# Differential attention: low weight parts made by an accumulating DMA, and one reciprocal for two sums

## The chip, the cores and the metric

The program runs on one core of a Trainium2 chip. The metric is the device time of one execution in microseconds (us), as the median of several. The engines are named as the profile names them: PE (TensorE, matrix products), DVE (VectorE), ACT (ScalarE), POOL (GpSimd) and SP (SyncE, which issues most DMAs). PEld is PE's loading of weights, which overlaps with its products.

## The reference, cut to what matters

The model has four layers over 512 latent and 256 context tokens of width 1024. A layer is a token mixer and a squared-ReLU MLP. The mixer of layer 1, the second, is differential attention, and the change is in it alone. It has 8 heads with two softmax maps each:

```
s1 = q1 @ k1.T * scale;  s2 = q2 @ k2.T * scale        # q, k with rotary positions for latent tokens
p  = softmax(s1) - lam * softmax(s2)                   # lam: one learned scalar
o  = p @ v                                             # v is 128 wide per head
y  = (rms_norm(o, subln_g) * (1 - lam_init)) @ w_o
```

Latent queries attend to all 768 keys, context queries to the 256 context keys. Everything is in float32.

## The kernel before, in words

**Products in two parts.** Each float32 operand is split into a high part (a cast to the matrix engine's 32-bit format fp32r) and a low part (what the cast left out), and a product is three products: high by high, high by low, low by high (`mm3g`, L147). `split` (L95) makes the parts: the ACT casts (`hi`, L96), and the DVE subtracts the high part from the source (`lo`, L97). Weights come from HBM into a raw buffer, issued by SP, and are then split (`wload` L99, and `gload` L111 with a pool of its own for four tiles `g`).

**The stage.** `diff` (L803) works on head after head. Its weights are loaded in tiles of 128x512. A pool of eight tiles (tag `w`) holds four pairs of parts; raw tiles have two buffers. The weights of a value projection (`gen_v`, L841, for two heads at a time) are four pairs, those of a key projection (`loads`, L895) two, those of the output projection (`gen_wo`, L911) four one after the other; those of a query projection go through `gload`. For each head and block of 128 queries `S` (L929) makes the scores of both maps in PSUM and then the softmax: the DVE takes the row maximum (L948), the ACT the exponential with its row sum `li` (L949), the DVE the reciprocal (L950) and its product with `lam` (L952); the ACT scales the second map (L953) and the DVE combines the two (L954). `Tr` transposes them, `PVa` and `PVb` multiply by the values and normalise.

**What sets the order.** PE's order is written out by hand. The object `Fill` (L163) holds the projections as generators in a queue (`v0`, `q1`, `k2`, ...), and between the steps of the attention `F(ns)` runs as many of their products as fit. `prime` (L184) starts the loads of the next generator in the queue early. A load takes the next buffers of the pool in turn, so it has to wait until the last product that reads the buffers' former tile. DVE, ACT, POOL and SP get their order from a scheduler when the program is built; each runs its instructions strictly in that order.

**Names.** `raw` is a weight as loaded, `whi`/`wlo` and `g` are its parts; `hhi`/`hlo` the parts of the normalised input; `pw` the PSUM tile of a projection; `qsw`, `qt` the rope steps (L867 to L870, one of them on the POOL); `kh`, `kl` the parts of the keys, of which `kh` is copied to a second place by a DMA of the POOL (L891); `x` the residual stream, into which `accum` (L368) adds a projection from PSUM.

Of the kernel before, what the change touches and what calls it, by code (L numbers as in the profile page):

```python
# [11 lines left out]
F32 = mybir.dt.float32  # L12
F32R = mybir.dt.float32r
BF16 = mybir.dt.bfloat16
AF = mybir.ActivationFunctionType
ALU = mybir.AluOpType
# [28 lines left out]
def body(ctx: ExitStack, tc, a, out):  # L45
    nc = tc.nc
# [25 lines left out]
    def phase(es, name, raw, psum, npb=None, rw=1024):  # L72
        state["rw"] = rw
        state["raw"] = pool(es, f"raw_{name}", raw)
        state["pp"] = pool(es, f"pp_{name}", 1, space=bass.MemoryType.PSUM)
        state["psum"] = psum
        state["np"] = pool(es, f"np_{name}", 1)
        state["npb"] = npb or {}
# [10 lines left out]
    def rawt():  # L89
        return state["raw"].tile([128, state["rw"]], F32, name="raw", tag="raw")  # L90

    def rd(t):
        return t.bitcast(F32)

    def split(hi, lo, src):  # L95
        nc.scalar.copy(hi, src)  # L96
        nc.vector.tensor_sub(lo, src, rd(hi))  # L97

    def wload(pl, src, n=None):  # L99
        raw = rawt()  # L100
        wd = state["rw"]
        n = n or wd
        nc.sync.dma_start(raw[:, :n], src)
        hi = pl.tile([128, wd], F32R, name="whi", tag="w")
        lo = pl.tile([128, wd], F32R, name="wlo", tag="w")
        split(hi[:, :n], lo[:, :n], raw[:, :n])
        return hi, lo

    pre = {}

    def gload(srcs, n=512):  # L111

        w = []
        for src in srcs:
            raw = rawt()
            nc.sync.dma_start(raw[:, :n], src)
            hi, lo = (gp.tile([128, 512], F32R, name="g", tag="g", bufs=4) for _ in range(2))
            split(hi[:, :n], lo[:, :n], raw[:, :n])
            w.append((hi, lo))
        return w  # L120

# [681 lines left out]
    def diff(l, h, nm):  # L803
        T = TT
        with ExitStack() as es:
            phase(es, "d", 2, {"s": (1024, 2), "u": (512, 2), "w": (512, 2)}, {"v": 1, "t": 1, "r": 1, "u": 1}, rw=512)
            cp = pool(es, "dc")
            wp = pool(es, "dw", 8)
            sp = pool(es, "ds")
# [9 lines left out]
            lam = cp.tile([128, 1], F32, name="lam")  # L819
            for i in range(2):  # L820
                nc.vector.scalar_tensor_tensor(
                    lj[:, 0:64], lam4[:, i * 128:i * 128 + 64], 1.0, lam4[:, i * 128 + 64:i * 128 + 128],
                    op0=ALU.mult, op1=ALU.mult, accum_out=ls[:, i:i + 1])
# [6 lines left out]
            scale = 64 ** -0.5  # L830
# [8 lines left out]
                    nc.gpsimd.tensor_copy(klz[i][m][o], zt[o])  # L839

            def gen_v(pr):  # L841
                wv = [wload(wp, a["dwv"][pr, i]) for i in range(4)]
                yield 0.0
                V[pr] = vh, vl = [sp.tile([128, 6, 256], F32R, name=n, tag="v", bufs=2) for n in ("vh", "vl")]
                for t0 in (0, 2, 4):
                    p = pt_("w")
                    for t in range(2):
                        i = 0
                        for k in range(KT):
                            hh, hl = tview(h[k], t0 + t)  # L850
                            wh, wl = tview(wv[k // 2], k % 2, 256)
                            for u_, v_ in ((hh, wh), (hh, wl), (hl, wh)):
                                mm(p[:, t * 256:(t + 1) * 256], u_, v_, i == 0, i == 23)
                                i += 1
                                yield 109.0
                    split(vh[:, t0:t0 + 2], vl[:, t0:t0 + 2], p.rearrange("p (t e) -> p t e", e=256))
# [16 lines left out]
            def put_q(hd):  # L873
                qs[hd] = [sp.tile([128, T], F32R, name=f"qs{m}", tag="qs", bufs=4) for m in range(2)]

                def put(t, c0, w_):
                    for m, (r, o) in enumerate(halves):
                        q = qs[hd][m][:, c0:c0 + w_]
                        nc.scalar.activation(q[r], t[r], AF.Copy, scale=scale)
                        nc.vector.scalar_tensor_tensor(q[o], t[r], scale, rd(q[r]), op0=ALU.mult, op1=ALU.subtract)  # L880
                return put

            def put_k(hd):
                kh[hd] = [sp.tile([128, T], F32R, name=f"kh{m}", tag="kh", bufs=4) for m in range(2)]
                kl[hd] = klz[hd % 2]

                def put(t, c0, w_):
                    for m, (r, o) in enumerate(halves):
                        q = kh[hd][m][:, c0:c0 + w_]
                        nc.scalar.copy(q[r], t[r])  # L890
                        nc.gpsimd.dma_start(q[o], q[r])  # L891
                        nc.vector.tensor_sub(kl[hd][m][r, c0:c0 + w_], t[r], rd(q[r]))  # L892
                return put

            def loads(src):  # L895
                return [wload(wp, src[i]) for i in range(2)]

            def gens(i, hd):

                st = []  # L900

                def piece(part):
                    if not st:
                        st.extend(((loads(a["dwk"][hd]), put_k(hd)) if i == 0 else
                                   (gload([a["dwq"][hd, j] for j in range(2)]), put_q(hd))))
                    yield 0.0
                    yield from proj(st[0], part, st[1])

                return [piece(part) for part in parts(T)]

            def gen_wo(pr, norm=None):  # L911
                ws = [wload(wp, a["dwo"][pr, b]) for b in range(2)]
                yield 0.0
                for b in range(4):
                    w = ws[b]
                    if b < 2:
                        ws.append(wload(wp, a["dwo"][pr, b + 2]))
                    for j in range(2):
                        p = pt_("w")
                        yield from mm3g(p, 2, lambda k: kview(w, k * 2 + j), lambda k: O[2 * pr + k], [(0, 512)])  # L920
                        accum(2 * b + j, 0, 512, p, l, G_A)
                    p = pt_("w")
                    for j in range(2):
                        yield from mm3g(p[:, j * 256:], 2, lambda k: kview(w, k * 2 + j), lambda k: O[2 * pr + k], [(512, 256)], off=512)
                        accum(2 * b + j, 512, 256, p[:, j * 256:(j + 1) * 256], l, G_A)
                        if norm:
                            norm.feed(2 * b + j)

            def S(hd, c0, qi, cqi=None):  # L929

                s = [pt_("s"), pt_("s")]
                rows = [(c0 + qi * 128, [(0, 512, 0), (512, 256, 512)], 0, T,
                         [sp.tile([128, T], F32, name=f"e{m}", tag=f"e{m}", bufs=2 - m) for m in range(2)])]
                if cqi is not None:
                    rows.append((SL + cqi * 128, [(SL, SC, 768)], T, SC, [nacc[:, 0:256], nacc[:, 256:512]]))
                for q0, bl, _, _, _ in rows:
                    for m in range(2):
                        for k0, kw, o0 in bl:
                            o = s[m][:, o0:o0 + kw]
                            mm(o, qs[hd][m][:, q0:q0 + 128], kh[hd][m][:, k0:k0 + kw], True, False)  # L940
                            mm(o, qs[hd][m][:, q0:q0 + 128], kl[hd][m][:, k0:k0 + kw], False, True)
                for _, _, o0, w_, e in rows:
                    ri = []
                    for m in range(2):
                        mx = sp.tile([128, 1], F32, name="mx", tag="mx", bufs=4)
                        li = sp.tile([128, 1], F32, name="li", tag="li", bufs=4)
                        sv = s[m][:, o0:o0 + w_]
                        nc.vector.reduce_max(mx, sv, axis=AX.X, negate=True)  # L948
                        nc.scalar.activation(e[m], sv, AF.Exp, bias=mx, accum_out=li)  # L949
                        nc.vector.reciprocal(li, li)  # L950
                        ri.append(li)
                    nc.vector.tensor_mul(ri[1], ri[1], lam)  # L952
                    nc.scalar.activation(e[1], e[1], AF.Copy, scale=ri[1])  # L953
                    nc.vector.scalar_tensor_tensor(e[0], e[0], ri[0], e[1], op0=ALU.mult, op1=ALU.subtract)  # L954
                return s, [r[4][0] for r in rows]

            def Tr(e, c0, qi, b):
# [70 lines left out]
            for hd in range(8):  # L1028
                p = hd // 2
                w = (5900, 3900, 7000, 7000, 7000, 7000, 7000, 5000)[hd]  # L1030
# [20 lines left out]
                st = PVa(hd, 0)  # L1051
# [10 lines left out]
                v = 0.5 * w if hd % 2 and hd < 6 else w  # L1062
# [5 lines left out]
                st = PVa(hd, 512)  # L1068
# [429 lines left out]
```

## Time and profile before

| what | value |
|---|---|
| median of 3 runs | 2881.78 us (2878.43 to 2882.46) |
| the profiled execution: its own time, its span | 2881.57 us, 2879.8 us |
| busy, share of the span: PE / PEld / DVE / ACT / POOL | 95% / 82% / 67% / 44% / 11% |
| chain that ended last, by engine | PE 78%, DVE 14%, ACT 4%, DMA 2%, issue 2%, POOL 1% |
| TensorE's granted clock, mean | 0.983 |
| DMAs issued by the POOL (queue q0) | 3.15 MB, 0.6% of 16 engines' span |

Busy shares are averages over layers that have different limits. The differential attention lies between about 740 and 1180 us of the span; the Fourier mixer and the first MLP are ahead of it, MLP, latent attention and the other layers behind. The chain is followed back from the last instruction, at each step to what released it. A row of the timeline gives start, duration, engine, line and operation; in square brackets stands how long the engine was idle before it and what ended that. The clock 1.0 is 2.4 GHz and 0.5 is 1.2 GHz; a mean between them is a mix of both.

### The profile page before, as it was taken

To read this page: it belongs to the slowest core of one execution; us is meant where nothing else is said; L and a number is where in the kernel's file an instruction comes from. 1 tells how busy PE (TensorE), PEld (TensorE's weight loads), DVE (VectorE), ACT (ScalarE), POOL (GpSimd) and SP (SyncE) were. 2 spreads that over 40 slices of the span, in tenths; PEclk is the share of its full clock that TensorE was granted. 3 is DMA by queue.
4 is the path that set the end of the run, shared out by engine and by line. 5 is a ranking of instruction groups with operands and counts; after the bars stand their busy time and mean duration, and the time that the engine had idled before them with its cause. 6 is when DMAs were issued, how large, how long until landed. Compare 5 with 4: busy or idle time off the path is not lost.

```text
span 2879.8 us, 39661 instructions
## 1 busy us (share of the span) xinstructions
PE 2736.4 (95%) x15387; PEld 2356.3 (82%) x15387; DVE 1925.4 (67%) x3371; ACT 1269.4 (44%) x2333; POOL 303.9 (11%) x235
## 2 busy tenths in 40 slices
PE   8999999999799989799999999899899999999998
PEld 5788888888778878688888897788788888888887
DVE  7986665657697778885555448999885656564344
ACT  4543222225475656533232235777544335543242
POOL 0010000002110100100000002756300001100001
PEclk9999999999899999899999999999999999999999
DMA  9454333322211111253333311111365541232231
GB/s 322 149 177 131 117 110 110 110 95 76 56 40 46 49 36 50 66 168 116 115 116 117 110 44 45 34 37 32 111 212 175 175 147 56 92 106 96 81 111 51
DMA packets 95452, 294.00 MB, mean 102 GB/s; under 512 B 11265, under 2 KB 15521, under 8 KB 94753
## 3 DMA queue, kind: packets, MB, share of 16 engines
q1 hardware_dynamic: 92704, 288.33, 31.5%
q0 software_dynamic: 2560, 3.15, 0.6%
q8 instruction: 121, 1.98, 0.3%
q14 instruction: 67, 0.54, 0.1%
HBM read 283.29 MB, written 2.11 MB: 99 GB/s over the span
## 4 chain that ended last, share of the span: by engine, by line
PE 78%; DVE 14%; ACT 4%; DMA 2%; issue 2%; POOL 1%; POOLq 0%; SPq 0%; ACTq 0%; DVEq 0%
PE pw L140 69%; PE pu L140 4%; PE ps L140 3%; DVE x L371 1%; DVE ptl L97 1%; PE pu L797 1%; DVE wlo L97 1%; DVE mx L948 1%; ACT e L1288 1%; DVE mx L1286 1%; DVE nu L328 1%; DVE hlo L330 1%; PE pn L140 0%; DVE hlo L348 0%; DMA raw<-in_w 0%
## 5 line engine op out<-in xcount | busy, mean ns | idle before, releaser
L96 ACT CAST whi<-raw 128x1024 fp32r<-128x1024 f32 (+1 forms) x322 | 308.4, 984 | 1070.6 <-PE pw L140 1013.3
L140 PE MATMUL pw<-hhi,wlo 128*128 128x512 f32 (+2 forms) x1680 | 587.1, 349 | 12.5 <-DVE wlo L97 12.5
L140 PE MATMUL pw<-hhi,whi 128*128 128x512 f32 (+2 forms) x1680 | 589.8, 351 | 1.7 <-DVE kl L892 1.0
L140 PE MATMUL pw<-hlo,whi 128*128 128x512 f32 (+2 forms) x1680 | 589.2, 351 | 0.0
L140 PE MATMUL pw<-ahi,whi 128*128 128x512 f32 (+1 forms) x1664 | 568.6, 342 | 0.1
L140 PE MATMUL pw<-alo,whi 128*128 128x512 f32 (+1 forms) x1664 | 567.3, 341 | 1.1 <-DVE alo L97 1.1
L140 PE MATMUL pw<-ahi,wlo 128*128 128x512 f32 (+1 forms) x1664 | 566.1, 340 | 0.0
L371 DVE SCALAR_TENSOR_TENSOR x<-pw,mod,x 128x512 f32<-128x512 f32 (+1 forms) x504 | 302.2, 622 | 288.7 <-PE pw L140 286.4
L97 DVE TENSOR_TENSOR wlo<-raw,whi 128x1024 fp32r<-128x1024 f32 (+1 forms) x322 | 362.4, 1141 | 165.1 <-ACT whi L96 163.6
L140 PEld LDWEIGHTS pw<-hhi,wlo 128*128 128x128 f32 x1680 | 318.4, 190 | 56.2 <-DVE wlo L97 13.1
L140 PEld LDWEIGHTS pw<-hhi,whi 128*128 128x128 f32 x1680 | 317.8, 189 | 46.2 <-DVE qt L868 1.6
L140 PEld LDWEIGHTS pw<-hlo,whi 128*128 128x128 f32 x1680 | 317.7, 189 | 42.7
L140 PEld LDWEIGHTS pw<-ahi,whi 128*128 128x128 f32 x1664 | 315.4, 190 | 37.4 <-ACT ahi L96 0.6
L140 PEld LDWEIGHTS pw<-alo,whi 128*128 128x128 f32 x1664 | 315.4, 190 | 37.2 <-DVE alo L97 1.6
L140 PEld LDWEIGHTS pw<-ahi,wlo 128*128 128x128 f32 x1664 | 315.1, 189 | 36.1
L264 DVE SCALAR_TENSOR_TENSOR raw<-raw,cb 128x1024 f32<-128x1024 f32 x176 | 214.9, 1221 | 114.8 <-DMA raw<-in_modw 113.2
L307 POOL TENSOR_TENSOR nacc<-nacc,nsq 128x256 f32<-128x256 f32 x70 | 53.0, 757 | 1751.8 <-ACT nsq L306 1751.5
L264 DVE SCALAR_TENSOR_TENSOR junk<-raw,cb 128x1024 bf16<-128x1024 f32 x96 | 118.8, 1238 | 71.6 <-DMA raw<-in_modw 69.3
L97 DVE TENSOR_TENSOR alo<-r,ahi 128x768 fp32r<-128x768 f32 (+2 forms) x134 | 105.9, 793 | 75.4 <-ACT ahi L96 75.1
L1290 POOL TENSOR_SCALAR e<-e,li 128x768 f32<-128x768 f32 x64 | 145.6, 2282 | 93.4 <-DVE li L1289 74.5
L97 DVE TENSOR_TENSOR ptl<-pu,pth 128x384 fp32r<-128x384 f32 (+1 forms) x208 | 106.1, 539 | 6.9 <-ACT pth L96 4.1
L140 PE MATMUL pw<-hhi,g 128*128 128x512 f32 (+2 forms) x384 | 99.4, 340 | 4.0 <-DVE x L371 2.9
(330 smaller groups left out, 4287.1 us busy)
## 6 DMA issues: line engine op xcount, KB each, us to landing
raw<-in_w SPq DMA_DIRECT2D x252, 512.0 KB, 4.0
raw<-in_modw SPq DMA_DIRECT2D x176, 512.0 KB, 3.7
wm<-in_msh SPq DMA_DIRECT2D x32, 256.0 KB, 6.4
raw<-in_fw SPq DMA_DIRECT2D x10, 512.0 KB, 4.6
cb<-scr SPq DMA_DIRECT2D x4, 1024.0 KB, 5.0
raw<-in_dwk SPq DMA_DIRECT2D x16, 256.0 KB, 2.7
raw<-in_dwq SPq DMA_DIRECT2D x16, 256.0 KB, 2.9
raw<-in_dwv SPq DMA_DIRECT2D x16, 256.0 KB, 2.8
```

Of the source, the lines that this page charges most:

```text
L96: nc.scalar.copy(hi, src)
L97: nc.vector.tensor_sub(lo, src, rd(hi))
L140: r = nc.tensor.matmul(o, lhsT, rhs, start=start, stop=stop)
L264: nc.vector.scalar_tensor_tensor(o, m, 1.0, cb[:, v * 1024:(v + 1) * 1024], op0=ALU.mult, op1=ALU.mult, accum_out=mcol(mod[l, ch], v, k))
L307: nc.gpsimd.tensor_tensor(nacc[:, c0:c0 + w], nacc[:, c0:c0 + w], s, op=ALU.add)
L328: nc.vector.scalar_tensor_tensor(u, xs, am, r, op0=ALU.mult, op1=ALU.mult)
L330: nc.vector.scalar_tensor_tensor(lo, u, sh, rd(hi), op0=ALU.add, op1=ALU.subtract)
L371: nc.vector.scalar_tensor_tensor(xs, src, mcol(mod[l, ch], 0 if c0 < SL else 1, n), xs, op0=ALU.mult, op1=ALU.add)
L797: nc.tensor.transpose(t[:, i * 128:(i + 1) * 128], p[:, (k0 + i) * 128:(k0 + i + 1) * 128], ident)
L948: nc.vector.reduce_max(mx, sv, axis=AX.X, negate=True)
L1286: nc.vector.reduce_max(mx, s[:, :T], axis=AX.X, negate=True)
L1290: nc.gpsimd.tensor_scalar(et, et, li, None, op0=ALU.mult)
```

## The change

1. `wload` and `gload` get a flag `far`. With it the parts are made by `split_far`: the ACT casts the high part, then writes the negated high part into the low tile, and a DMA of the POOL adds the raw tile onto it. The raw tile is so read until that DMA has landed. The flag is set for the weights of all value and output projections, of the key projections of heads 2 to 7 and of the query projections of heads 1 to 7: 58 loads in all. The first weights (`wk0`, `wq0`, `wk1`) are split as before.
2. Raw tiles of the stage have three buffers instead of two.
3. The sums of both maps go into two columns of one tile, and one reciprocal of 128x2 takes the place of two of 128x1.

```diff
+    def split_far(hi, lo, raw):
+        nc.scalar.copy(hi, raw)
+        nc.scalar.activation(lo, rd(hi), AF.Copy, scale=-1.0)
+        nc.gpsimd.dma_start(rd(lo), raw, accum_op=ALU.add)
...
-            phase(es, "d", 2, {"s": (1024, 2), "u": (512, 2), "w": (512, 2)}, {"v": 1, "t": 1, "r": 1, "u": 1}, rw=512)
+            phase(es, "d", 3, {"s": (1024, 2), "u": (512, 2), "w": (512, 2)}, {"v": 1, "t": 1, "r": 1, "u": 1}, rw=512)
...
-                wv = [wload(wp, a["dwv"][pr, i]) for i in range(4)]
+                wv = [wload(wp, a["dwv"][pr, i], far=True) for i in range(4)]
...
-                        st.extend(((loads(a["dwk"][hd]), put_k(hd)) if i == 0 else
-                                   (gload([a["dwq"][hd, j] for j in range(2)]), put_q(hd))))
+                        st.extend(((loads(a["dwk"][hd], True), put_k(hd)) if i == 0 else
+                                   (gload([a["dwq"][hd, j] for j in range(2)], far=True), put_q(hd))))
...
-                ws = [wload(wp, a["dwo"][pr, b]) for b in range(2)]
+                ws = [wload(wp, a["dwo"][pr, b], far=True) for b in range(2)]
...
-                    ri = []
+                    li = sp.tile([128, 2], F32, name="li", tag="li", bufs=4)
                     for m in range(2):
...
-                        nc.scalar.activation(e[m], sv, AF.Exp, bias=mx, accum_out=li)
-                        nc.vector.reciprocal(li, li)
-                        ri.append(li)
-                    nc.vector.tensor_mul(ri[1], ri[1], lam)
-                    nc.scalar.activation(e[1], e[1], AF.Copy, scale=ri[1])
-                    nc.vector.scalar_tensor_tensor(e[0], e[0], ri[0], e[1], op0=ALU.mult, op1=ALU.subtract)
+                        nc.scalar.activation(e[m], sv, AF.Exp, bias=mx, accum_out=li[:, m:m + 1])
+                    nc.vector.reciprocal(li, li)
+                    nc.vector.tensor_mul(li[:, 1:2], li[:, 1:2], lam)
+                    nc.scalar.activation(e[1], e[1], AF.Copy, scale=li[:, 1:2])
+                    nc.vector.scalar_tensor_tensor(e[0], e[0], li[:, 0:1], e[1], op0=ALU.mult, op1=ALU.subtract)
```

The scheduler orders DVE, ACT, POOL and SP anew; line numbers of the changed kernel are 12 higher from L109 on (10 higher behind the softmax).

The DVE at the start of the stage, before: the low parts of the second head's key weight (wlo_6618, wlo_6624) stand behind the rope and query steps of the first head.

```order
L870 TENSOR_TENSOR qt_6605<-qt_6605,qsw_6606 128x512
L330 SCALAR_TENSOR_TENSOR hlo_1750<-big_6572,mod1_0_101,hhi_1749 128x256
L330 SCALAR_TENSOR_TENSOR hlo_1752<-big_6576,mod1_0_101,hhi_1751 128x256
L880 SCALAR_TENSOR_TENSOR qs0_6484<-qt_6605,qs0_6484 64x512
L880 SCALAR_TENSOR_TENSOR qs1_6485<-qt_6605,qs1_6485 64x512
L97 TENSOR_TENSOR wlo_6618<-raw_6615,whi_6617 128x512
L97 TENSOR_TENSOR wlo_6624<-raw_6621,whi_6623 128x512
L867 STREAM_SHUFFLE qsw_6653<-pw_6627 128x512
```

The DVE at the same place with the change: both stand around the first rope step (the shuffle of qsw_6526), long before the rows above.

```order
L97 TENSOR_TENSOR wlo_6491<-raw_6488,whi_6490 128x512
L97 TENSOR_TENSOR wlo_6497<-raw_6494,whi_6496 128x512
L342 SCALAR_TENSOR_TENSOR hlo_1752<-nu_6394,mod1_0_101,hhi_1751 128x256
L97 TENSOR_TENSOR wlo_6618<-raw_6615,whi_6617 128x512
L833 SCALAR_TENSOR_TENSOR big_6462,ls_6463<-big_6460 128x64
L840 TENSOR_SCALAR gs_6470<-pb_88 128x1
L833 SCALAR_TENSOR_TENSOR big_6462,ls_6463<-big_6460 128x64
L837 TENSOR_TENSOR lam_6464<-ls_6463 128x1
L879 STREAM_SHUFFLE qsw_6526<-pw_6500 128x512
L838 TENSOR_SCALAR lam_6464<-lam_6464 128x1
L97 TENSOR_TENSOR wlo_6624<-raw_6621,whi_6623 128x512
```

So the two low parts moved ahead of the first head's rope, past the normalisation of the context tokens.

The ACT around the second value projection, before: casts of its third and fourth weight (whi_7871, whi_7877) among the key copies kh.

```order
L287 ACTIVATE nt_7832<-nr_7831 128x256
L96 CAST whi_7871<-raw_7869 128x512
L890 CAST kh0_7656<-qt_7845 64x512
L890 CAST kh1_7657<-qt_7845 64x512
L96 CAST whi_7877<-raw_7875 128x512
L96 CAST oh_7557<-nu_7819 128x256
L890 CAST kh0_7656<-pw_7881 64x256
```

The ACT at that place with the change (the same two weights are whi_7857 and whi_7864):

```order
L299 ACTIVATE nt_7816<-nr_7815 128x256
L114 CAST whi_7857<-raw_7855 128x512
L115 ACTIVATE wlo_7858<-whi_7857 128x512
L902 CAST kh0_7644<-qt_7829 64x512
L902 CAST kh1_7645<-qt_7829 64x512
L96 CAST oh_7545<-nu_7803 128x256
L114 CAST whi_7864<-raw_7862 128x512
L902 CAST kh0_7644<-pw_7869 64x256
L115 ACTIVATE wlo_7865<-whi_7864 128x512
```

Each cast is followed by a negation (L115), the fourth weight's with a key copy between the two.

The POOL at the first value projection with the change: its four accumulations (wlo_6796 to wlo_6817) between the key copies of the second head; before, only the key copies and rope products stood in this queue. SP issues the fourth load, raw_6814, into the buffer that raw_6793 had.

```order
L903 DMA kh0_6486<-kh0_6486 64x512
L903 DMA kh1_6487<-kh1_6487 64x512
L116 DMA wlo_6796<-raw_6793 128x512
L116 DMA wlo_6803<-raw_6800 128x512
L116 DMA wlo_6810<-raw_6807 128x512
L903 DMA kh0_6486<-kh0_6486 64x256
L903 DMA kh1_6487<-kh1_6487 64x256
L116 DMA wlo_6817<-raw_6814 128x512
```

The accumulations joined the queue; the last stands behind the context tokens' key copies.

## Rows read from the trace of the kernel before

**Rows 1.** Stretches: from:to and length, busy by engine (instructions), granted clock, DMA share, GB/s.
```profile
core 0: us, PE busy (x) PEld busy (x) DVE busy (x) ACT busy (x) POOL busy (x), PEclk, DMA share, GB/s
...
740.00:1180.00 440.00, 395.47 (x2513) 350.14 (x2511) 340.23 (x723) 266.29 (x597) 35.14 (x44) 0.97 0.17 44
...
727.00:739.00 12.00, 0.10 (x1) 0.00 (x0) 11.84 (x24) 6.33 (x13) 2.60 (x3) 0.66 0.11 22
739.00:745.00 6.00, 5.62 (x14) 4.48 (x15) 0.92 (x2) 0.00 (x0) 0.00 (x0) 0.54 0.31 87
...
804.00:810.00 6.00, 5.22 (x23) 4.55 (x24) 4.88 (x10) 2.78 (x7) 0.00 (x0) 0.72 0.16 55
```

**Rows 2.** Waits of PE, 756 to 1222 us: total, times, longest.
```profile
PE pw L140 <- DVE x L371: 23.0, 22, 2.2
...
PE ps L140 <- DVE qs L880: 2.7, 2, 2.4
```

**Rows 3.** Timeline at the start: start, duration, engine, instruction [idle before, ended by].
```profile
738.63 1.29 DVE L97 TENSOR_TENSOR wlo<-raw,whi 128x512 fp32r<-128x512 f32 x2
...
739.38 0.79 PE L140 MATMUL pw<-hhi,wlo 128*128 128x512 f32 x1 [12.27 <-DVE wlo L97]
...
751.70 0.62 ACT L96 CAST whi<-raw 128x512 fp32r<-128x512 f32 x1
...
760.72 0.28 PE L140 MATMUL pw<-wlo,hhi 128*128 128x256 f32 x1
...
763.76 0.50 PE L140 MATMUL ps<-kh,qs 128*128 128x512 f32 x1 [1.93 <-ACT nacc L949]
...
765.56 0.80 PE L140 MATMUL ps<-kh,qs 128*128 128x512 f32 x1 [0.83 <-ACT nacc L949]
```

**Rows 4.** Groups, 740 to 1180 us: busy us, mean ns | idle before, by whom.
```profile
L949 ACT ACTIVATE e<-ps,mx 128x768 f32<-128x768 f32 x64 | 57.9, 904 | 47.7 <-DVE mx L948 47.1 <-PE pw L140 0.4
...
L97 DVE TENSOR_TENSOR wlo<-raw,whi 128x512 fp32r<-128x512 f32 x44 | 30.0, 685 | 8.8 <-ACT whi L96 8.6
...
L96 ACT CAST whi<-raw 128x512 fp32r<-128x512 f32 x44 | 27.2, 624 | 19.8 <-PE pw L140 12.7 <-DMA raw<-in_dwk 3.4 <-DMA raw<-in_dwo 2.0
...
L891 POOL DMA_DIRECT2D kh<-kh x30 | 15.8, 526 | 39.0 <-ACT kh L890 36.5 <-PE ps L140 1.8
...
L950 DVE RECIPROCAL li<-li 128x1 f32<-128x1 f32 x96 | 14.6, 156 | 8.1 <-ACT e L949 5.7 <-ACT nacc L949 1.7
...
L97 DVE TENSOR_TENSOR g<-raw,g 128x512 fp32r<-128x512 f32 x16 | 11.0, 685 | 0.6 <-ACT g L96 0.3
```

**Rows 5.** DMA issues: engine, count, KB each, median us from issue to landing.
```profile
raw<-in_w SPq DMA_DIRECT2D x252, 512.0 KB, 4.0
...
raw<-in_dwv SPq DMA_DIRECT2D x16, 256.0 KB, 2.8
...
kh<-kh POOLq DMA_DIRECT2D x16, 128.0 KB, 3.5
...
kh<-kh POOLq DMA_DIRECT2D x16, 64.0 KB, 2.3
```

**Rows 6.** Timeline, fourth weight of the value projections 2, 3 and 4.
```profile
858.90 0.62 ACT L96 CAST whi<-raw 128x512 fp32r<-128x512 f32 x1
...
861.34 0.39 PE L140 MATMUL pw<-wlo,hhi 128*128 128x256 f32 x1 [0.40 <-DVE wlo L97]
...
973.35 0.62 ACT L96 CAST whi<-raw 128x512 fp32r<-128x512 f32 x1
...
975.40 0.38 PE L140 MATMUL pw<-wlo,hhi 128*128 128x256 f32 x1 [0.99 <-DVE wlo L97]
...
1087.83 0.62 ACT L96 CAST whi<-raw 128x512 fp32r<-128x512 f32 x1
...
1089.88 0.38 PE L140 MATMUL pw<-wlo,hhi 128*128 128x256 f32 x1 [0.99 <-DVE wlo L97]
```

**Rows 7.** Timeline, third weight of the first output projection.
```profile
909.46 0.63 ACT L96 CAST whi<-raw 128x512 fp32r<-128x512 f32 x1
...
915.14 0.39 PE L140 MATMUL pw<-oh,wlo 128*128 128x512 f32 x1
```

More of the change, by code (lines that the diff above doesn't have):

```diff
@@ L97, in split, with wload @@
         nc.vector.tensor_sub(lo, src, rd(hi))
-    def wload(pl, src, n=None):
+    def wload(pl, src, n=None, far=False):
         raw = rawt()
@@ L105, in wload, with gload @@
         lo = pl.tile([128, wd], F32R, name="wlo", tag="w")
-        split(hi[:, :n], lo[:, :n], raw[:, :n])
+        if far:
+            split_far(hi[:, :n], lo[:, :n], raw[:, :n])
+        else:
+            split(hi[:, :n], lo[:, :n], raw[:, :n])
         return hi, lo
+    def split_far(hi, lo, raw):
+        nc.scalar.copy(hi, raw)
+        nc.scalar.activation(lo, rd(hi), AF.Copy, scale=-1.0)
+        nc.gpsimd.dma_start(rd(lo), raw, accum_op=ALU.add)
     pre = {}
-    def gload(srcs, n=512):
+    def gload(srcs, n=512, far=False):
         w = []
@@ L117, in gload @@
             hi, lo = (gp.tile([128, 512], F32R, name="g", tag="g", bufs=4) for _ in range(2))
-            split(hi[:, :n], lo[:, :n], raw[:, :n])
+            if far:
+                split_far(hi[:, :n], lo[:, :n], raw[:, :n])
+            else:
+                split(hi[:, :n], lo[:, :n], raw[:, :n])
             w.append((hi, lo))
@@ L893, in put_k, with loads @@
                 return put
-            def loads(src):
-                return [wload(wp, src[i]) for i in range(2)]
+            def loads(src, far=False):
+                return [wload(wp, src[i], far=far) for i in range(2)]
             def gens(i, hd):
@@ L916, in gen_wo @@
                     if b < 2:
-                        ws.append(wload(wp, a["dwo"][pr, b + 2]))
+                        ws.append(wload(wp, a["dwo"][pr, b + 2], far=True))
                     for j in range(2):
@@ L942, in S @@
                 for _, _, o0, w_, e in rows:
-                    ri = []
+                    li = sp.tile([128, 2], F32, name="li", tag="li", bufs=4)
                     for m in range(2):
                         mx = sp.tile([128, 1], F32, name="mx", tag="mx", bufs=4)
-                        li = sp.tile([128, 1], F32, name="li", tag="li", bufs=4)
                         sv = s[m][:, o0:o0 + w_]
                         nc.vector.reduce_max(mx, sv, axis=AX.X, negate=True)
-                        nc.scalar.activation(e[m], sv, AF.Exp, bias=mx, accum_out=li)
-                        nc.vector.reciprocal(li, li)
-                        ri.append(li)
-                    nc.vector.tensor_mul(ri[1], ri[1], lam)
-                    nc.scalar.activation(e[1], e[1], AF.Copy, scale=ri[1])
-                    nc.vector.scalar_tensor_tensor(e[0], e[0], ri[0], e[1], op0=ALU.mult, op1=ALU.subtract)
+                        nc.scalar.activation(e[m], sv, AF.Exp, bias=mx, accum_out=li[:, m:m + 1])
[3 more added lines that the diff above has]
+                    nc.vector.scalar_tensor_tensor(e[0], e[0], li[:, 0:1], e[1], op0=ALU.mult, op1=ALU.subtract)
                 return s, [r[4][0] for r in rows]
```

## The prediction

> **What bounds the kernel now.** I read the table of stretches first, since the change touches only the second layer (differential attention, from about 740 to 1180 us). There the TensorE (PE) is busy 395.5 of 440 us, the DVE 340.2, the ACT 266.3 and the POOL 35.1 [rows 1]. So PE sets the end and 44.5 us is all its idle time. PE's order is written out by hand and the same before and after: whatever makes it wait is added to the end, unless a later wait shrinks by as much. The list of waits, restricted to PE, says for whom it waits: 23.0 us in 22 pieces (756 to 1222 us) are for the DVE's accumulation into x, which empties PSUM behind the output projection [rows 2]. One big hole lies ahead of these: at 739.38 PE has been idle for 12.27 us for a low weight part that the DVE computes from 738.63 on [rows 3]; in that hole the DVE is busy 11.84 of 12 us [rows 1]. That part stands late in the DVE's order, not late in its data.
>
> **What leaves the DVE.** 58 of the 60 subtractions in the groups of the stage (44 of wlo, 14 of the 16 of g; the two others belong to the next layer's first weight) at 0.685 us [rows 4] are 39.7 us. Two reciprocals become one of two columns: 48 of 96 go, at 0.156 us [rows 4], 7.5 us. Together 47 of 340 us, 14%. Little of it is on the path: PE's waits on the DVE end with an accumulation, a transposed block or a rope step, and I found removed instructions directly ahead of only some of them. 14% of the 23.0 us is 3.2. I take a gain of 3 us, ends: a loss of 4 (ACT, below) and a gain of 11.5 (half of the 23.0).
>
> **What it puts on the ACT and the POOL.** 58 negations, priced as the cast of the same shape at 0.624 us [rows 4], are 36.2 us: ACT goes from 266 to about 302 of 440 us, above the DVE's new 293. No wait of PE on ACT in the list is long enough for me to price more than the 4 us named as an end. The POOL issues 58 more DMAs. An issue of 64 rows takes 0.526 us [rows 4]; at once or twice that for 128 rows they are 31 to 61 us beside 35 busy now, so it stays far from full. Behind a waiting issue stand the key copies and the rope product; in the order they come from the same projections, after the weights, so I cost this at nothing, with 6 us as the upper end inside the range.
>
> The rows show the issue taking one duration under a DVE that is busy 77% of the time [rows 1, 4]. The Trainium skill (SBUF — State Buffer, Summary: rules for kernel authors) warns against this place: software descriptor generation is starved while the DVE is in its two-port modes, so such a DMA should not be hidden under the DVE. If that held here, each issue would stretch by up to one DVE instruction. The 30 issues of the stage average 0.526 us, so the trace does not bear it out, and it gets no term.
>
> **The unknown: L, from issue to landing of an accumulating 256 KB DMA.** No row shows one. The POOL's plain copies land after 2.3 us (64 KB) and 3.5 us (128 KB); SP's loads after 2.8 us (256 KB) and 4.0 us (512 KB) [rows 5]. The lower end is 2.3. The upper is 7.0, twice the 128 KB row for twice the bytes. Against that row there are 128 KB more to move and the target to be read too, about one more 256 KB, which between the two loads costs 1.2 us: 4.7, and I take 4.5.
>
> By the fit in the Trainium skill (DMA: Bandwidth & Descriptors, Anatomy of one DMA — SWDGE path: about 2.0 us plus the bytes over 436 GB/s) it would be 2.6 us, an estimate from that page, and the sum would come near the rival with the short landing. The same fit gives 2.3 us for the 128 KB copies whose row says 3.5, so the trace speaks against it.
>
> **Where L is on the path.** The load is called far because it is issued early, but it can't be split before the buffers of an earlier weight are free. For the third and fourth pair of a value weight these are the buffers of the key projection that runs directly ahead. In the trace the fourth pair's cast starts at 858.90, 973.35 and 1087.83 and PE takes the low part at 861.34, 975.40 and 1089.88, each time after waiting for it (the first time 0.40, then 0.99 and 0.99 us) [rows 6]. Cover is gone there already. In the new ACT order a key copy stands between cast and negation at the first, and two copies and a square at the others, which take the time before the cast today. The negation thus ends at about 860.5, 974.0 and 1088.9, and the low part lands L + 0.1 later. Against PE's use that is L - 0.7, L - 1.3 and L - 0.9 more wait: 3L - 2.9 in all, 10.6 us at 4.5. Loads of queries and keys, and the first pairs, have many microseconds in hand.
>
> The output projection's third pair is nearest to them: cast at 909.46, low part used at 915.14 [rows 7]. With 0.63 for the cast and 0.62 for the negation it lands at 910.8 + L, L - 4.3 late. There are two such places: 0.4 us at 4.5.
>
> New waits also cost clock. After a wait of 2.4 us [rows 2] the stretch from 804 to 810 shows a granted clock of 0.72 [rows 1], a mix of the levels 2.4 and 1.2 GHz: 0.28 of 6 us is 1.7 us lost. Three waits of 3 to 4 us make 5 us (ends 0 and 8).
>
> **The start.** With a third raw buffer and the DVE order shown, the low part that PE waited for is ready before its projection, so the hole of 12.27 us goes, with the low clock behind it (0.54 from 739 to 745 [rows 1]). Late next: the DVE, which was full through the hole and still has to empty PSUM for the context projections. I put these 8 us earlier, not 12. The first value cast, at 751.70 today [rows 3], comes at 743.7. Its raw buffer is the one the fourth value load needs (three buffers, four loads), and the buffer is now held until the accumulation has read it. So the chain is: 743.7, cast and negation 1.2, landing L, load 2.8 [rows 5], cast 0.6, three exponentials of the first scores that stand there in ACT's order (at most 0.9 each, 2.7 [rows 4]), negation 0.6, landing L: 751.6 + 2L. PE uses that part at 760.72 today [rows 3]. Meanwhile the softmax has caught up and the waits of 1.93 and 0.83 us behind it [rows 3] go. The start is worth 2L - 9.1 - 2.8 = 2L - 11.9: -2.9 at 4.5. Most of the hole is thus given back at once.
>
> **Sum** at L = 4.5: start -2.9, value weights +10.6, output weight +0.4, clock +5, DVE relief -3: +10.1 us. The profiled execution took 2881.57 us (its span 2879.8 and 1.8 around it), 0.2 below the median 2881.78; the sum gives 2891.7, and I say 2891.
>
> **Rivals.**
> *Short landing.* The accumulation lands as the 64 KB copies do, L = 2.3: start -7.3, value weights +4.0, output 0, one slow clock stretch +1.7, relief -3: -4.6, or 2877, no change that can be told. For it: a load of 256 KB lands after 2.8. Against it: the 128 KB copies.
> *The DVE's queue sets the pace* (the faster side). PE's waits on the accumulation into x fall by half, -11.5, because every step that empties PSUM stands in one queue that gets 14% shorter; L = 2.9, between the two copies: start -6.1, value +5.8, clock +1.7: -10.1, or 2871. It decides from a relief of about 8 us on, with L below 3. For it: 23.0 us of waits with one name. Against it: in the output projection's stretch few of the removed instructions stand ahead of these waits.
> *Long landing.* L = 7, the read of the target and a shared queue doubling the copy: start +2.1, value +18.1, output +5.4, clock +7, relief -3: +29.6, or 2911.
>
> **How the numbers follow.** Two executions can be told apart from about 0.2%, 5.8 us. Forecast (L from 3.5 to 5.8, so +4 to +20, 2885 to 2902) 0.57, a tenth of it in the band of no change; long landing 0.12; short landing 0.14; DVE's queue 0.17, taken as faster with a little of the short landing. Faster 0.20, same 0.22, slower 0.58. The range for 8 in 10 runs from 2872 to 2909.
>
> **What would show it.** The DMA table should give a median of 3.5 to 5.8 us for wlo<-raw. PE's waits should list the DMA of wlo, some 3 to 4 us each, at the first block of value weights 2 to 4, and one of several microseconds at the start in place of the 12.27. The wait on x should stay at 20 or so. The DVE should be near 293 us in the stage and ACT near 302. I am wrong if the accumulations land in under 3 us, if the hole at the start goes and nothing follows it, or if the waits on x halve.

## The result, and the profile after

The changed kernel takes 2906.97 us, median of 4 runs (2903.68 to 2910.35), against 2882.12 us for the kernel before: 24.9 us more, ratio 1.009 with a 95% interval of 1.0077 to 1.0103. The forecast was 2891 in a range of 2872 to 2909. The profiled execution, the longest of the four, took 2910.35 us, its span 2908.4; against the 2879.8 of before that is 28.6 us, and the traces are compared on that basis.

The stage between 740 and 1180 us, and two of the stretches of [rows 1], in the changed kernel. Columns as there.

```profile
core 0: us, PE busy (x) PEld busy (x) DVE busy (x) ACT busy (x) POOL busy (x), PEclk, DMA share, GB/s
740.00:1180.00 440.00, 378.67 (x2366) 336.12 (x2367) 285.12 (x579) 277.40 (x613) 85.40 (x100) 0.95 0.35 75
727.00:739.00 12.00, 9.47 (x50) 7.66 (x49) 11.87 (x25) 5.46 (x11) 2.85 (x4) 1.00 0.12 23
...
862.00:868.00 6.00, 5.78 (x38) 5.78 (x39) 2.13 (x3) 1.36 (x3) 0.00 (x0) 0.73 0.15 44
984.00:990.00 6.00, 5.88 (x31) 5.50 (x32) 2.24 (x4) 2.00 (x5) 0.00 (x0) 0.66 0.15 45
1111.00:1117.00 6.00, 5.45 (x21) 5.06 (x22) 1.95 (x3) 1.98 (x4) 0.00 (x0) 0.50 0.23 57
...
960.00:966.00 6.00, 5.82 (x24) 5.03 (x25) 2.08 (x5) 2.56 (x7) 0.60 (x1) 0.72 0.42 87
1087.00:1093.00 6.00, 5.66 (x23) 4.82 (x24) 2.13 (x5) 2.62 (x7) 0.76 (x1) 0.72 0.39 90
1148.00:1154.00 6.00, 5.38 (x30) 5.27 (x31) 5.76 (x14) 5.12 (x12) 1.38 (x1) 0.72 0.18 52
```

The first row shows less work done in the same 440 us: PE 378.7 busy instead of 395.5, with 2366 products instead of 2513. The DVE fell from 340 to 285 and PE became idler all the same. The second row is the place of the old hole: PE is busy 9.47 of 12 us where it had 0.10. The next three, behind the waits for value weights, have a granted clock of 0.73, 0.66 and 0.50, a mix of the two levels and at last the lower one; the same stretches of before (from 861, 975 and 1090 us there) have 1.00. The last three stand behind other waits, told below.

PE's waits in the stage, changed kernel (756 to 1250 us): total, times, longest.

```profile
PE pw L152 <- DVE x L383: 22.9, 23, 2.2
PE pw L152 <- DMA wlo<-raw: 18.3, 8, 4.8
PE pu L809 <- DVE ptl L97: 13.5, 9, 2.8
PE pu L152 <- DVE ptl L97: 6.7, 10, 1.2
```

The same view of before, the two rows that answer to the last two:

```profile
PE pu L797 <- DVE ptl L97: 4.4, 4, 1.7
...
PE pu L140 <- DVE ptl L97: 3.0, 5, 0.7
```

The wait for x is 22.9 us against 23.0 [rows 2]: 14% less work on the DVE bought nothing there. The 18.3 us for accumulations were forecast in the main. The third and fourth rows were not: the waits for `ptl`, the low parts of the transposed softmax blocks, went from 7.4 to 20.2 us.

PE's waits for the fourth value weights and its four longest for `ptl`, from the changed kernel's timeline (idle before and what ended it in brackets):

```profile
760.80 0.58 PE L152 MATMUL pw<-wlo,hhi 128*128 128x256 f32 x1 [4.84 <-DMA wlo<-raw]
...
862.23 0.58 PE L152 MATMUL pw<-wlo,hhi 128*128 128x256 f32 x1 [3.05 <-DMA wlo<-raw]
...
960.18 0.55 PE L809 MATMUL pu<-ident,e 128*128 128x128 f32 x3 [2.76 <-DVE ptl L97]
...
984.12 0.58 PE L152 MATMUL pw<-wlo,hhi 128*128 128x256 f32 x1 [3.94 <-DMA wlo<-raw]
...
1019.83 0.55 PE L809 MATMUL pu<-ident,e 128*128 128x128 f32 x3 [2.30 <-DVE ptl L97]
...
1087.34 0.90 PE L809 MATMUL pu<-ident,e 128*128 128x128 f32 x3 [2.63 <-DVE ptl L97]
...
1111.55 0.58 PE L152 MATMUL pw<-wlo,hhi 128*128 128x256 f32 x1 [4.24 <-DMA wlo<-raw]
...
1148.62 0.69 PE L809 MATMUL pu<-ident,e 128*128 128x128 f32 x2 [2.58 <-DVE ptl L97]
```

PE's order is the same in both kernels, so each product can be set beside its twin. The first value projection's last weight is used at 760.80 against 760.72 [rows 3]: the hole's 12.27 us are given back by then. The fourth weights of the others are used at 862.23, 984.12 and 1111.55 against 861.34, 975.40 and 1089.88 [rows 6], so 0.9, 8.7 and 21.7 us late. Their own waits grew by 2.65, 2.95 and 3.25 us, 8.9 together; the rest of the delay arises between them, where the forecast had the slow clock and nothing else.

How it arises shows in the chain of work that ended last, followed through 20 us of the changed kernel (start, duration, what):

```profile
1005.47 3.40 DMA wlo<-raw
...
1008.93 5.25 DMA raw<-in_dwk
...
1014.25 0.62 ACT whi L114
1014.87 0.38 ACT nt L296
1015.25 0.53 ACT wlo L115
...
1016.06 3.31 DMA wlo<-raw
...
1019.42 2.72 DMA raw<-in_dwq
```

And the ACT in the same place:

```profile
1009.24 0.37 ACT L995 COPY nu<-pu 128x256 f32<-128x256 f32 x1
1014.25 0.62 ACT L114 CAST whi<-raw 128x512 fp32r<-128x512 f32 x1 [4.64 <-DMA raw<-in_dwk]
1014.78 0.47 ACT L296 ACTIVATE nt<-pu,epst 128x256 f32<-128x256 f32 x1
...
1017.88 0.90 ACT L960 ACTIVATE e<-ps,mx 128x768 f32<-128x768 f32 x1 [1.36 <-DVE mx L959]
```

An accumulation is issued at 1005.47 and lands 3.40 us later. Only then is its raw buffer free, and 0.07 us later SP issues the load of a key weight into it. The load takes 5.25 us, beside two more accumulations and a second load. PE needs that weight later, and none of its waits on accumulations is for a key weight; but its cast stands in ACT's order ahead of the norm step (L296) and of the next exponential, and ACT stands still 4.64 us before it. The DVE stands behind it in turn:

```profile
1015.28 0.42 DVE L297 TENSOR_SCALAR nv<-pu 128x256 f32<-128x256 f32 x1 [7.74 <-ACT nt L296]
...
1016.90 0.95 DVE L959 TENSOR_REDUCE mx<-ps 128x1 f32<-128x768 f32 x1
```

It idles 7.74 us for the norm step, with the row maximum (L959) behind; the exponential starts at 1017.88. The cast ahead of `ptl` stands behind it on ACT and `ptl` itself behind the row maxima on the DVE, so PE waits for `ptl` until 1019.83. So a weight that PE was not waiting for held up the softmax.

### The profile page after: what moved, and what is told of

Its sections match the earlier page's. It is cut to its first block, busy times and chain, and to the rows that moved or that the text cites. A ratio compares the mean times of both kernels' runs of the same rounds, so it can differ in the third digit from the quotient of the medians.

```text
span 2908.4 us, 39763 instructions
## 1 busy us (share of the span) xinstructions
PE 2748.4 (95%) x15387; PEld 2366.3 (81%) x15387; DVE 1888.0 (65%) x3265; ACT 1298.0 (45%) x2391; POOL 356.6 (12%) x293
## 4 chain that ended last, share of the span: by engine, by line
PE 75%; DVE 11%; issue 5%; ACT 4%; DMA 4%; POOL 1%; POOLq 0%; SPq 0%; ACTq 0%; DVEq 0%
PE pw L152 66%; PE pu L152 4%; PE ps L152 3%; DVE x L383 1%; DMA wlo<-raw 1%; DVE ptl L97 1%; PE pu L809 1%; DVE mx L959 1%; ACT e L1298 1%; DVE mx L1296 1%; DVE wlo L97 1%; DVE hlo L342 1%; DVE nu L340 1%; DVE hlo L360 0%; DMA raw<-in_dwq 0%
## 5 line engine op out<-in xcount | busy, mean ns | idle before, releaser
L96 ACT CAST whi<-raw 128x1024 fp32r<-128x1024 f32 (+1 forms) x278 | 281.2, 1041 | 1052.7 <-PE pw L152 983.8
L97 DVE TENSOR_TENSOR wlo<-raw,whi 128x1024 fp32r<-128x1024 f32 (+1 forms) x278 | 333.1, 1216 | 155.8 <-ACT whi L96 155.6
L97 DVE TENSOR_TENSOR ptl<-pu,pth 128x384 fp32r<-128x384 f32 (+1 forms) x208 | 106.2, 540 | 15.4 <-ACT pth L96 12.8
```

## Experiments

Each ratio is against runs of the kernel before on the same chip, in brackets the 95% interval. "Far" is the flag of the accumulating DMA.

### The DVE adds in place of the DMA

```
-        nc.gpsimd.dma_start(rd(lo), raw, accum_op=ALU.add)
+        nc.vector.tensor_add(lo, raw, rd(lo))
```

> The changed kernel, but the DVE adds the raw weight onto the negated high part (0.69 us) where the accumulating DMA did: ACT keeps its 58 negations and raw its three buffers, only the landing is gone. Theory (the time went into landings: 20.0 us of PE waits on accumulations, and 12.8 us more of waits for blocks of ptl, because a raw buffer is held until the landing, the next load comes late, and ACT's cast of it stands in order ahead of the softmax): no PE wait on wlo of over 1 us, waits on ptl back to about 8 us, time 2868 to 2880. Rival A (the 36 us of negations on ACT delay the softmax, whoever adds): waits on ptl stay at 18 to 20 us, time 2882 to 2888.

2876.24 us, 0.9989 [0.9981, 0.9998]. PE's waits in the stage:

```profile
PE pw L152 <- DVE x L383: 23.5, 23, 2.2
PE pw L152 <- DVE wlo L116: 7.1, 4, 2.6
PE pu L152 <- DVE ptl L97: 6.2, 9, 1.2
PE pu L809 <- DVE ptl L97: 5.0, 5, 1.7
```

ACT does all the casts and negations of the changed kernel (298 us busy of 440), the DVE is as loaded as in the kernel before (340), and about 1.0% of the time is back. The waits for `ptl` fall to 11.2 us, so ACT's load accounts for at most 4 of the 12.8 us that they grew by. One part of the expectation failed: waits on wlo of up to 2.6 us are left, since the negation on ACT, then an addition on the DVE, is one step more behind a cast that was already late.

### Value weights by subtraction

```
-                wv = [wload(wp, a["dwv"][pr, i], far=True) for i in range(4)]
+                wv = [wload(wp, a["dwv"][pr, i]) for i in range(4)]
```

> The changed kernel, but the 16 value weights are split as before (DVE subtraction); the 42 other loads keep the accumulation. Theory: the PE waits on accumulations at the four value projections go (17 of 20.0 us) with the low clock behind three of them (about 5 us), the waits on ptl stay between 8 and 20; 2880 to 2892. Rival A (ACT's load): ACT loses 10 of its 36 us, and PE's waits on the accumulations go likewise, but ptl stays at 20; 2885 to 2890, so this run does not part the two. Rival B (the wait comes back elsewhere: in x or in ptl, since PE is ahead of the softmax): 2898 or more.

2883.71 us, 1.0012 [1.0002, 1.0023]. The waits for accumulations go; 16.9 us of waits for `ptl` stay (11.1 and 5.8):

```profile
PE pw L152 <- DVE x L383: 23.0, 23, 2.4
PE pu L809 <- DVE ptl L97: 11.1, 8, 2.6
...
PE pu L152 <- DVE ptl L97: 5.8, 10, 1.1
```

So the value weights are about 0.8% of the time, and the second cause does not hang on them.

### Four raw buffers, and the control

```
-            phase(es, "d", 3, ...
+            phase(es, "d", 4, ...
-                t = sp.tile([128, 512], F32, name="qt", tag="qt", bufs=2)
+                t = sp.tile([128, 512], F32, name="qt", tag="qt", bufs=1)
```

> The changed kernel with four raw buffers instead of three; for the room the rope tile qt has one buffer instead of two. All accumulations stay. Theory: loads no longer wait for the landing before them, so ACT's waits on raw (37 us in the stage) fall below 15, PE's waits on ptl from 20.2 to about 8, the start's 4.84 us wait shrinks, and the waits at value weights 2 to 4 (3.0 to 4.4 us each) stay, since those hang on the pool of parts: 2886 to 2898. Rival A (ACT's load): ptl stays, 2903 to 2910.

2895.84 us, 1.0055 [1.0041, 1.0069].

```profile
PE pw L152 <- DVE x L383: 23.2, 22, 2.3
PE pw L152 <- DMA wlo<-raw: 16.5, 8, 4.4
...
PE pu L152 <- DVE ptl L97: 5.7, 8, 1.1
PE pu L809 <- DVE ptl L97: 4.6, 5, 1.7
```

With one raw buffer more, ACT's waits for raw fall from 31 to 9 us and PE's for `ptl` from 20.2 to 10.3, while the accumulations, the negations and most of PE's waits on accumulations are still there (at the start the longest falls from 4.84 to 1.86 us). That separates the two causes. But the scheduler also orders ACT anew in places, and the key weight's cast shown above now comes ahead of the copies before it; the run with plain copies below keeps the order. The second line of the edit alone:

> The changed kernel with one buffer for the rope tile qt and still three raw buffers: the control of the run with four raw buffers. Theory: 2903 to 2912, ptl waits stay at 18 to 22. Rival (the gain with four raw buffers came from the rope tile): 2890 to 2899.

2908.32 us, 1.0091 [1.0077, 1.0105], waits for `ptl` 20.3 us: the rope tile has no part in it.

### Three raw buffers alone, one reciprocal alone, and both

> The kernel before with three raw buffers instead of two and nothing else. Theory: the hole of 12.27 us goes, the DVE gives some of it back in the context projections and the first softmax; 7 us remain, 2872 to 2878. Rival C (the DVE was full there, all of it is given back): 2880 to 2884.

2873.55 us, 0.9979 [0.9971, 0.9988]: of the 12.27 us about 6 remain.

> The kernel before with the one 128x2 reciprocal for both maps and nothing else (raw two buffers, all parts by subtraction). Theory (relief of the DVE is worth nothing, since PE's 25 us of waits on x did not shrink where the DVE lost 60 us): within 0.2% of before, waits on x 24 to 26. Rival (the DVE's queue sets the pace): 7.5 us less DVE work shorten the waits on x by 2 or more, 2874 to 2878. Rival (the first map's scale factor now waits for the second map's exponential): slower by 2 to 6 us.

2881.83 us, 1.0 [0.9991, 1.0009], with 23.0 us of waits for x, as before [rows 2]: 48 instructions less on the DVE, and nothing gained or lost.

> Three raw buffers and one reciprocal, all low parts by subtraction: the change without its accumulating DMAs. Theory: the time of raw 3 alone, 2869 to 2876, the hole at the start stays closed, and the whole loss of the change (31 to 36 us from here) is the accumulations'. Rival (the negation and accumulation gave something elsewhere): above 2878.

2873.21 us, 0.9962 [0.9948, 0.9975]: the change without its accumulating DMAs. It is the shortest of the kernels tried against its runs of before, and faster than both kernels of this study. From the three buffers alone it can't be told apart, since the two intervals overlap.

### A plain copy in place of the accumulation

```
-        nc.gpsimd.dma_start(rd(lo), raw, accum_op=ALU.add)
+        nc.gpsimd.dma_start(rd(lo), raw)
```

> The changed kernel with plain copies raw to lo in place of the accumulations (left out: the addition, so the low parts are the weights themselves). Reading 1 (an accumulation costs the reading of its target): alone in its queue the 256 KB land after 2.3 to 2.9 us instead of 3.3, the waits at value weights 2 to 4 shrink by 0.4 to 1 us each, the time by 3 to 8 us. Reading 2 (the copy of 256 KB between tiles takes this by itself): 3.2 to 3.4 us and the same time within 0.2%.

2892.25 us, 1.0038 [1.0024, 1.0051]. DMA issues of the changed kernel in the stage (count, KB each, median us from issue to landing):

```profile
wlo<-raw POOLq DMA_DIRECT2D x42, 256.0 KB, 3.4
...
g<-raw POOLq DMA_DIRECT2D x14, 256.0 KB, 3.3
```

With plain copies:

```profile
wlo<-raw POOLq DMA_DIRECT2D x44, 256.0 KB, 2.3
g<-raw POOLq DMA_DIRECT2D x14, 256.0 KB, 2.3
```

Accumulating costs 1.0 us over copying (reading 1), and its least is 3.2 where the copy's is 2.2. The time came down by 15 us, twice as far as expected, and not where it was expected: the waits at value weights 2 to 4 are 2.60, 4.58 and 4.10 us, 11.3 together as against 11.2 (3.05, 3.94 and 4.24), since PE now comes to them up to 0.9 us earlier in relation to the DMA's issue. The microsecond is also taken off every hold of a raw buffer, and there it told: the waits for `ptl` fell from 20.2 to 11.6 us. ACT, at the key weight shown above:

```profile
998.89 0.62 ACT L114 CAST whi<-raw 128x512 fp32r<-128x512 f32 x1 [1.03 <-DMA raw<-in_dwk]
```

It stands still 1.03 us there instead of 4.64. DVE, ACT, POOL and SP have the changed kernel's order in this run, instruction for instruction, so here no new order can be the reason: the shorter landing alone removed 8.6 of the 12.8 us of waits for `ptl` that the change had added.

### Accumulations only where there is room, against none

> Accumulations kept only where both causes are out of the way: four raw buffers (qt has one), and the third and fourth pairs of the value weights and all of the first value projection split by the DVE; the other 48 loads keep them. Theory: no PE wait on an accumulation over 1 us, waits on ptl 8 to 12, waits on x still 24 to 26, since a relief of the DVE is worth nothing to them; 2870 to 2880, no faster than the same kernel without accumulations. Rival (the relief of 40 us of DVE work shows once the landings are hidden): 3 us or more below that kernel.

> Four raw buffers, one qt, one reciprocal, all parts by subtraction: the comparison for the run beside it. Theory: as with three raw buffers, 2869 to 2877, since loads were not late there. Rival (a fourth buffer helps the first projections): 2864 to 2868.

2876.87 us, 0.9981 [0.9972, 0.9989], with 48 accumulations; 2876.22 us, 0.9987 [0.9979, 0.9996], without. With accumulations, the waits and the stage:

```profile
PE pw L152 <- DVE x L383: 23.2, 22, 2.3
```

```profile
740.00:1180.00 440.00, 393.59 (x2520) 347.11 (x2520) 318.69 (x645) 296.88 (x658) 79.99 (x93) 0.98 0.34 74
```

Without:

```profile
PE pw L152 <- DVE x L383: 23.9, 23, 2.4
```

```profile
740.00:1180.00 440.00, 393.89 (x2513) 348.04 (x2511) 346.30 (x689) 270.42 (x606) 36.95 (x45) 0.97 0.17 46
```

With both causes out of the way the accumulations cost nothing, and a DVE with 28 us less to do in the stage gains nothing: the two ratios differ by less than the width of either interval.

## Why the prediction was right, and where not

Right in its sign and range, and in that the landings at the value weights cost more than the hole gave. The size was not: the sum gave 10.1 us more, and 24.9 were measured; and that not because of L. The time alone lies nearest the rival with the long landing (2911), whose L = 7 was not found. That 2907 is still inside the range is partly luck, since most of what brought it there was not among the costs that were priced. By the prediction's own shares (0.57 less a tenth of it, and 0.12), slower should have had 0.63 and not 0.58.

- **The start.** Forecast 2L - 11.9, -2.9 at L = 4.5. Ahead of the second value projection the changed kernel leads by 1.8 us (0.89 late at 862.23, less the 2.65 us by which that wait grew). The hole went, and the fourth load waited for the first accumulation, as described: PE's 4.84 us at 760.80. That the chain ended at 760.75, where 751.6 + 2L gives 760.6, is luck: both landings were 1.1 us shorter than assumed (3.38), the first cast came 1.1 us later (744.83), the fourth load took 0.9 longer (3.72), and the rest was lost between the steps.
- **L.** Forecast 4.5, with a median of 3.5 to 5.8 as its sign; the median is 3.4; it is 3.2 to 3.3 where nothing else is in flight, and up to 5.8 behind other accumulations. My step from 128 to 256 KB took the 3.5 us of the key copies as an effect of size. It was what else was in flight: in the changed kernel the 128 KB copies have a median of 2.4 and the 64 KB ones 3.2, and in the kernel before the 128 KB copies with no load in flight (825.49 and 826.12) took 2.20 and 2.45 us, those beside two loads 3.7 to 4.3. So the "short landing" is the time of the plain copy, and the rest is the accumulation.
- **Value weights.** Forecast 10.6 of wait and 5 of slow clock. The three waits grew by 8.9, and the clock of the 6 us behind them (0.73, 0.66, 0.50) is 1.6 + 2.0 + 3.0 = 6.6. Together 15.5 against 15.6: the mechanism held, and with the landings at these places (3.73, 4.02 and 4.33) L - 0.7, L - 1.3 and L - 0.9 make 9.2 of wait; but that the total agrees is luck, 1.7 less wait and 1.6 more clock. The run without far value weights shows the cause.
- **Output weights.** Forecast 0.4; the list has one wait of 0.36 us at such a weight, and nothing more.
- **The DVE's relief.** Forecast 3 gained; nothing. Four kernels agree: the changed one, the one with a single reciprocal, the DVE's additions, and accumulations with room have 22.9, 23.0, 23.5 and 23.2 us of waits for x, whatever the DVE's load. In the changed kernel PE's waits for e, qs and qt shrank by 2.7 us together; with the DVE's additions, which give the DVE its work back, they shrank as much, so this is not the relief either.
- **The step that failed:** "Loads of queries and keys, and the first pairs, have many microseconds in hand." They have, for PE: of its ten waits on accumulations nine are for value weights and one for an output weight. I asked when the product needs the weight and not what else stands behind its cast on ACT. Waits for `ptl` grew by 12.8 us, and three stretches of 6 us behind such waits (from 960, 1087 and 1148 us) have a clock of 0.72, 1.7 us each: some 18 us that the sum didn't have. I had priced the held raw buffer at the start of the stage alone; it holds at every load. Four raw buffers bring the time down by 11 us, about 2 of them at the start.

The terms as measured: -1.8 for everything ahead of the second value projection, which holds 2.6 of the growth for `ptl` and the shrinking for e and qs already; behind it +8.9 and +6.6 at the value weights, +10.1 for `ptl` (6.4 to 16.5) and +5.1 of clock. They make 28.9 against 28.6 between the spans. So close a fit is partly luck, since PE was not working through all of the slow stretches, and small waits that grew or shrank by about a microsecond are left out.

What stays open: whether the negations alone, with no DMA behind them, would cost ACT's neighbours a few microseconds. The run with the DVE's additions is 0.27% behind three buffers with one reciprocal, on another chip and with intervals of 0.09 and 0.13% to either side, and its 4.7 us of additional waits for wlo point that way.

## What to carry to other kernels

When work moves from an engine to a DMA, two times count: when the result lands, and how long its source stays held. The second sets the issue of the next load; and a load that is early enough for its product can still be late for the instruction that converts it, which stands in an in-order queue ahead of urgent work. Before relieving an engine, check that a wait on it shrinks when its load does: here 7 to 47 us less work on the DVE left the waits for x where they were.

## What the runs showed of the hardware

- An accumulating DMA of 256 KB between tiles, issued by the POOL, lands after 3.2 to 3.3 us when nothing else is in flight (17 of 19 cases in the changed kernel); the plain copy of the same bytes takes 2.2 to 2.3 (23 of 26). Size mattered less than company: 64 KB copies had medians of 2.3 and 3.2 us in two kernels.
- Loads beside accumulations land later: 2.6 us is the key weights' median, 5.25 took the one beside two accumulations (issued 1006.65 and 1008.29; the second took 5.65 us itself) and another load. In the kernel before, without accumulations, no weight load of this layer took more than 3.63 us, those beside other loads included.
- The POOL's issue of a 128-row accumulation takes 0.89 us in the mean, of a plain copy of the same tile 0.56, of a 64-row copy 0.53 before and 0.60 in the changed kernel. The DVE was busy for 65% of the stage meanwhile (285 of 440 us).
